# One transformer block on one core: value subtractions and filler stores on GpSimd, the convolution's last columns placed directly, pools reordered, the output bank in halves

## The chip, the cores and the metric

The kernel runs on one core of one Trainium2 chip. The metric is the device time of one execution in microseconds; the time before is the median of three runs. The engines are called by the profile's names: PE (TensorE, its weight loads as PEld), DVE (VectorE), ACT (ScalarE), POOL (GpSimd) and SP (SyncE, which here only issues DMAs). ACT and POOL can issue DMAs too; a DMA instruction stands in its engine's queue like any other.

## The reference

One layer of a hybrid encoder block for a sequence of 1024 tokens and 1024 channels, everything in float32:

```
h = rmsnorm(x, ln1_g) * (1 + sc1) + sh1          # sc1, sh1, ... from silu(c) @ ada_w + ada_b
q, k, v, cb, cc, cx, ga, gb = split(h @ w_in)
q, k = rmsnorm per head of 64 channels           # 16 heads
y_a = stick_breaking_attention(q, k, v)          # causal, blocks of 128 queries
      # A[t,s] = sigmoid(z_ts) * prod_{s<j<t} (1 - sigmoid(z_tj)),  z = q.k / 8,  s < t;  y_a = A @ v
y_b = cb * causal_dwconv3(cc * cx, conv_w)
merged = sigmoid(ga) * (y_a @ w_branch_a) + sigmoid(gb) * (y_b @ w_branch_b)
x = x + g1 * (merged @ w_out)
h = rmsnorm(x, ln2_g) * (1 + sc2) + sh2
x = x + g2 * ((silu(h @ w_gate) * (h @ w_up)) @ w_down)
```

## The kernel before

**Arithmetic.** Every float32 operand of a product is split into a high part (a copy by ACT into the type fp32r) and a low part (source minus high part, by DVE), and each product is three matmuls: high-high, high-low, low-high. The gate, FFN and down projections use a Strassen-like scheme of seven products.

**Stages.** Modulation and the first norm with the first value projection; keys; the gate and convolution inputs (`gates`, L478), whose results go to DRAM (`d_sga`, `d_sgb`, `d_y`); the attention stage, which the change is about (from about 578 to 1058 us); branch A's projection; output projection and second norm; FFN; down projection.

**The attention stage.** It interleaves two streams on the same engines.

*Attention* (`attention`, L815) walks 16 heads times 8 query blocks. A step does `att_scores` (z = q.k by two matmuls, L763 and L764; sigmoid by ACT into the tile pt, L765; running product by a DVE scan, L769); the step before it does `att_trans` (PE transposes, L784; high part by ACT, L787; low part by DVE, L788); three steps after the scores, every second step does `att_av` (L792: matmuls with the value tile into the bank `o`, L799 and L800; ACT adds the last value column, L804; DVE combines, L806; SP stores `d_ya`, L808). The product uses differences of neighbouring values: `att_load` (L698) loads q and k parts for one head and, for an even head, the value columns twice, once shifted by a row (`va` and `vb`, one buffer each, L712), always for the head after the current one. `att_dv` (L716) subtracts them on DVE (L720), copies the high part into `vt` by ACT (L723) and makes the low part by DVE (L724); `vt` has two buffers. `load_vlast` (L726) loads the last value rows, 16 heads in two goes, into a tile that shares the buffer of `va`; `turn_vlast` transposes it.

*Fillers* (`fillers`, L855) are matmul work that attention doesn't need at once: the value projection of heads 8 to 15 (two times eight items, stored to `d_v` by ACT, L875); 16 convolution items (m, n), m a block of 128 channels and n a half of the sequence (load `y` from `d_y`, L883; 24 matmuls; DVE multiplies, L889; high and low part, L892 and L893; ACT stores both to `d_yb`, L894 and L895); then all of `d_yb` is read back into four large buffers `yh`, `yl` (16 DMAs of 512 KB, L902 and L903); and 16 items of branch B's projection (load `sb` from `d_sgb`, L908; 24 matmuls; DVE multiplies, L915; ACT stores `d_mb`, L916). `y` and `mb` share three buffers, `sb` has two, the high and low parts two each.

**What sets the order.** The program is traced in Python and a scheduler then fixes the order of each engine's instructions from a simulated timeline, by priority (attention is traced under `tc.high_priority()`) and readiness. `fill` (L926) traces fillers in proportion to the attention traced so far. `tc.issue_after(ins)` adds an order without a wait: what is traced inside comes after `ins` on the engine of `ins`. Each engine works through its order strictly one after the other. `reuse_waits="tile"` means that a buffer is reused as soon as the tile in it is released. The large buffers `big()` (four) hold the normed input `hh`, `hl` and later `yh`, `yl`. Tile pools are opened and closed like a stack, so a pool's tiles lie where an earlier pool's tiles were, in the order in which their tags first appear; pool `phb` (L693) holds the attention tiles.

Of the kernel before, what the change touches and what calls it, by code (L numbers as in the profile page):

```python
# [8 lines left out]
F32 = mybir.dt.float32  # L9
F32R = mybir.dt.float32r  # L10
AF = mybir.ActivationFunctionType
ALU = mybir.AluOpType
# [4 lines left out]
P = 128  # L17
T = 1024
D = 1024
KT = D // P  # L20
H = 16
DH = 64
# [6 lines left out]
def block_kernel(tc, x, x_t, cols, ada_1, ada_2, ada_row, w_q, w_kv, w_v1, w_cg, w_a, w_b, w_o, w_g, w_u, w_d, out):  # L29
    nc = tc.nc  # L30
# [7 lines left out]
    def nm(s):  # L38
        uid[0] += 1
        return f"{s}_{uid[0]}"  # L40

    def big():
        return bigp.tile([P, KT, 512], F32R, tag="big", bufs=4, name=nm("big"))
# [24 lines left out]
    d_v = [drp.tile([T + 1, n], F32, name=f"d_v{n}_{e}") for e, n in enumerate((512, 256, 256))]  # L68
    d_yb = [[drp.tile([P, KT, 512], F32, name=f"d_yb{e}{n}") for n in range(2)] for e in range(2)]
    d_ya = [drp.tile([P, KT, 512], F32, name=f"d_ya{n}") for n in range(2)]  # L70
    d_sga = drp.tile([KT, P, T], F32, name="d_sga")
    d_sgb = drp.tile([KT, P, T], F32, name="d_sgb")
    d_y = drp.tile([KT, P, T], F32, name="d_y")
    d_mb = drp.tile([KT, P, T], F32, name="d_mb")
# [58 lines left out]
    def tt(eng, out, a, b, op):  # L133
        eng.tensor_tensor(out=out, in0=a, in1=b, op=op)  # L134
# [3 lines left out]
    pps = psA.enter_context(tc.tile_pool(name="psA", bufs=1, space=PSUM, reuse_waits="tile"))  # L138
# [123 lines left out]
                             start=True, stop=True)  # L262

    split_hi(0)
    hh = [big() for n in range(2)]
    hl = [big() for n in range(2)]

    def norm_x(k, *n):
        src = xt(k, *n)
# [159 lines left out]
    for cc in (1, 2):  # L429
        w = wq[4:] if cc == 1 else [load_w(w_kv[cc, j]) for j in range(4)]  # L430
# [255 lines left out]
    pps = psB.enter_context(tc.tile_pool(name="psB", bufs=1, space=PSUM, reuse_waits="tile"))  # L686
# [4 lines left out]
    fq = fqpool.enter_context(tc.tile_pool(name="phg", bufs=1, side="right", reuse_waits="tile"))  # L691
    s3 = ExitStack()
    bp = s3.enter_context(tc.tile_pool(name="phb", bufs=1, reuse_waits="tile"))  # L693

    NPT = 5
    pts = [ptp.tile([P, D], F32, name=f"pt{j}") for j in range(NPT)]

# [18 lines left out]
    def att_dv(h):  # L716

        va, vb = vab
        if h % 2 == 0:
            tt(nc.vector, vb, vb, va, ALU.subtract)  # L720
        dv = vb[:, :, h % 2 * DH:h % 2 * DH + DH]
        vt = vts[h] = bp.tile([P, KT, P], F32R, tag="vt", bufs=2, name=nm("vt"))
        nc.scalar.activation(vt[:, :, :DH], dv, AF.Copy)  # L723
        tt(nc.vector, vt[:, :, DH:], dv, vt[:, :, :DH].bitcast(F32), ALU.subtract)  # L724

    def load_vlast(e):  # L726

        vl = bp.tile([8, 512], F32, tag="va", bufs=1, name=nm("vl"))
        for d, c in (((0, 0),), ((1, 0), (2, 256)))[e]:
            nc.sync.dma_start(vl[:, c:c + d_v[d].shape[1]], d_v[d][1:].rearrange("(i p) d -> i p d", p=P)[:, P - 1])  # L730
        return vl
# [10 lines left out]
    lastz = [None]  # L742
    lastld = [None]
    npt = [0]
    ats = {}
    ptof = {}

# [44 lines left out]
    def att_av(h, g):  # L792
        pr, e0 = h // 2, (h % 2) * DH
        vt = vts[h]
        o = pps.tile([P, 256], F32, tag="o", bufs=1, name=nm("o"))
        for j in range(2 * g + 2):
            c0 = P if j == 2 * g + 1 else 0
            th, tl = ats[h, g, j // 4]
            nc.tensor.matmul(o[:, c0:], vt[:, j, :], th[:, j % 4, c0:], start=(j == 0), stop=False)  # L799
            lastav[0] = nc.tensor.matmul(o[:, c0:], vt[:, j, :], tl[:, j % 4, c0:], start=False, stop=(j == 2 * g + 1))  # L800
        tmp = bp.tile([DH, 256], F32, tag="otmp", bufs=1, name=nm("otmp"))
        yv = bp.tile([DH, 256], F32, tag="oy", bufs=2, name=nm("oy"))
        for e in range(2):
            nc.scalar.activation(tmp[:, e * P:(e + 1) * P], o[:DH, e * P:(e + 1) * P], AF.Identity,  # L804
                                 bias=vlast[:, h, 2 * g + e:2 * g + e + 1])
        nc.vector.tensor_tensor(out=yv, in0=o[DH:], in1=tmp, op=ALU.add)  # L806
        hf, c0 = g // 2, (g % 2) * 256
        nc.sync.dma_start(d_ya[hf][e0:e0 + DH, pr, c0:c0 + 256], yv)  # L808
        yield (2 * g + 2) * 0.22

    NZ, NTR, NPJ, DAV, KQ = 2, 3, 2, 3, 2
# [30 lines left out]
    def load_ch(src):  # L842
        raw = g_raw(src)
        return g_split(raw[:, :512]), g_split(raw[:, 512:])
# [10 lines left out]
    def fillers():  # L855
        for e in range(2):
            w = []
            for j in range(2):
                with tc.issue_after(lastld[0].ins) if e else ExitStack():
                    raw = g_raw(w_v1[e, j])  # L860
                w += [g_split(raw[:, :512]), g_split(raw[:, 512:])]
            for i in range(8):
                n, t0 = i // 4, (i % 4) * P
                ps = ps_f()[:, :256]
                for k in range(KT):
                    if k == 4:
                        yield 1.3
                    wh, wl = (v[:, (k % 2) * 256:(k % 2) * 256 + 256] for v in w[k // 2])
                    sh, sl = hh[n][:, k, t0:t0 + P], hl[n][:, k, t0:t0 + P]
                    nc.tensor.matmul(ps, sh, wh, start=(k == 0), stop=False)  # L870
                    nc.tensor.matmul(ps, sh, wl, start=False, stop=False)
                    nc.tensor.matmul(ps, sl, wh, start=False, stop=(k == KT - 1))
                vs = fq.tile([P, 256], F32, tag=("ybh", "ybl")[i % 2], bufs=2, name=nm("vs1"))
                nc.scalar.activation(vs, ps, AF.Copy)
                nc.scalar.dma_start(d_v[1 + e][1 + i * P:1 + (i + 1) * P], vs)  # L875
                yield 1.3
        cb_w = {}
        for m, n in [(m, n) for m in range(KT - 2) for n in range(2)] + [(m, n) for n in range(2) for m in (KT - 2, KT - 1)]:
            if n == 0:
                cb_w[m] = load_ch(w_cg[0, m])  # L880
            w = cb_w[m]
            y = fp.tile([P, 512], F32, tag="st", bufs=3, name=nm("cy"))
            nc.sync.dma_start(y, d_y[m, :, n * 512:(n + 1) * 512])  # L883
            ps = ps_f()
            for kk in range(0, KT, KQ):
                if kk:
                    yield 0.65 * KQ
                mm_ch(ps, w, hh[n], hl[n], kk, kk + KQ)
            nc.vector.tensor_tensor(out=y, in0=ps, in1=y, op=ALU.mult)  # L889
            yh = fq.tile([P, 512], F32R, tag="ybh", bufs=2, name=nm("ybh"))  # L890
            yl = fq.tile([P, 512], F32R, tag="ybl", bufs=2, name=nm("ybl"))
            nc.scalar.activation(yh, y, AF.Copy)  # L892
            nc.vector.tensor_tensor(out=yl, in0=y, in1=yh.bitcast(F32), op=ALU.subtract)  # L893
            nc.scalar.dma_start(d_yb[0][n][:, m, :], yh.bitcast(F32))  # L894
            nc.scalar.dma_start(d_yb[1][n][:, m, :], yl.bitcast(F32))  # L895
            yield 0.65 * KQ
        yh, yl = [], []
        for n in range(2):
            yh.append(big())
            yl.append(big())  # L900
            for k in range(0, KT, 2):
                nc.sync.dma_start(yh[n][:, k:k + 2].bitcast(F32), d_yb[0][n][:, k:k + 2])  # L902
                nc.sync.dma_start(yl[n][:, k:k + 2].bitcast(F32), d_yb[1][n][:, k:k + 2])  # L903
        for m in range(KT):
            w = load_ch(w_b[m])
            for n in range(2):
                sb = fp.tile([P, 512], F32, tag="sgi", bufs=2, name=nm("sgi"))
                nc.sync.dma_start(sb, d_sgb[m, :, n * 512:(n + 1) * 512])  # L908
                ps = ps_f()
                for kk in range(0, KT, KQ):  # L910
                    if kk:
                        yield 0.65 * KQ
                    mm_ch(ps, w, yh[n], yl[n], kk, kk + KQ)
                mb = fp.tile([P, 512], F32, tag="st", bufs=3, name=nm("mb"))
                nc.vector.tensor_tensor(out=mb, in0=ps, in1=sb, op=ALU.mult)  # L915
                nc.scalar.dma_start(d_mb[m, :, n * 512:(n + 1) * 512], mb)  # L916
                yield 0.65 * KQ

    FILL = 2.5 * 16 * 5.2
# [14 lines left out]
    with tc.high_priority():  # L934
        vl = load_vlast(0)
# [38 lines left out]
    for n in range(2):  # L974
        for k in range(KT):
            yr = fp.tile([P, 512], F32, tag="yr", bufs=2, name=nm("yr"))
            nc.sync.dma_start(yr, d_ya[n][:, k, :])
            tag, bufs = slots[n * KT + k]
# [6 lines left out]
    for m in range(KT):  # L985
        if m == KT - 1:
            split_wo(g_raw(w_o[0]), cpa, 1, ("c00", "c10", "c01", "c11"))
        w = load_ch(w_a[m])
        for n in range(2):
            sa = fp.tile([P, 512], F32, tag="sgi", bufs=2, name=nm("sgi"))  # L990
            nc.sync.dma_start(sa, d_sga[m, :, n * 512:(n + 1) * 512])
            mb = fp.tile([P, 512], F32, tag="st", bufs=3, name=nm("mb"))
# [17 lines left out]
    pps = psD.enter_context(tc.tile_pool(name="psD", bufs=1, space=PSUM, reuse_waits="tile"))  # L1010
# [404 lines left out]
    vt = [e2.tile([P, 512], F32, name=f"vt{t}") for t in range(4)]  # L1415
# [101 lines left out]
    for t in range(4):  # L1517
        for e, c, ps in ((nc.sync, slice(0, 256), pa[3]), (nc.scalar, slice(256, 512), pa[7])) if t == 3 else (
                (nc.sync, slice(0, 512), pa[t]),):
            nc.vector.scalar_tensor_tensor(out=vt[t][:, c], in0=ps[:, :c.stop - c.start], scalar=gmod[:, 1, t:t + 1],  # L1520
                                           in1=u2t[t][:, c], op0=ALU.mult, op1=ALU.add)
# [60 lines left out]
```

## Time and profile before

| | before |
|---|---|
| time, median of 3 runs | 1875.63 us (1875.41 to 1878.0) |
| the profiled execution | 1874.59 us, span 1872.5 us |
| mean granted TensorE clock | 0.991 |
| busy: PE / PEld / DVE / ACT / POOL | 1813.7 / 1503.2 / 1343.1 / 777.7 / 415.5 us |
| chain that ended last | PE 76%, DVE 11%, DMA 6%, issue 3%, ACT 2%, POOL 1% |
| DMA bytes | 351.94 MB, mean 188 GB/s |

The span is the time from the first to the last instruction of the profiled execution. "Busy" is the time in which an engine had an instruction under way; a row of the profile names the line, the engine, the operation, the tile written and the tiles read, the count, the busy time, the mean duration in ns, and the time that the engine stood idle before these instructions with what ended it. A name with a q (ACTq, SPq) is the engine's queue: there DMAs and semaphore waits appear.

### The profile page before, as it was taken

What the parts mean: (1) busy time and instruction counts of PE and PEld (TensorE: products, weight loads), DVE (VectorE), ACT (ScalarE), POOL (GpSimd) and SP (SyncE); (2) the same over time, 40 slices, a digit from 0 to 9 for tenths busy, and PEclk for the clock granted to TensorE, in tenths of its full rate; (3) what the DMA queues carried; (4) which work ended last, traced back from release to release, by engine and by line L of the source; (5) the groups of instructions that cost most, each with busy time, mean ns of one, the idle gap of its engine ahead of it and who ended that gap; (6) DMA issues with size and microseconds to landing.
All of it is one profiled execution on the core that took longest, in us unless ns stands there. A gap on an engine that the chain in (4) does not pass through costs nothing.

```text
span 1872.5 us, 24605 instructions
## 1 busy us (share of the span) xinstructions
PE 1813.7 (97%) x8765; PEld 1503.2 (80%) x8765; DVE 1343.1 (72%) x1896; ACT 777.7 (42%) x1462; POOL 415.5 (22%) x292
## 2 busy tenths in 40 slices
PE   7999999999999999988999999999999999999999
PEld 4787778887788988877888788877888888888787
DVE  6873877779953878877788554489997778643953
ACT  4342553333333656555556322244444344422320
POOL 1043328323420000000000001336554545300000
PEclk9999999999999999998999999999999999999999
DMA  9598452228638575667663544514454344299776
GB/s 388 198 309 307 162 176 77 76 93 292 227 123 251 134 189 163 185 191 250 168 167 95 195 131 158 169 57 169 147 191 147 135 154 172 102 347 327 247 234 216
DMA packets 154112, 351.94 MB, mean 188 GB/s; under 512 B 15211, under 2 KB 54397, under 8 KB 151814
## 3 DMA queue, kind: packets, MB, share of 16 engines
q1 hardware_dynamic: 96336, 239.54, 40.3%
q10 hardware_dynamic: 56646, 107.16, 15.7%
q0 software_dynamic: 1008, 3.67, 0.5%
q8 instruction: 70, 1.15, 0.3%
q14 instruction: 52, 0.43, 0.1%
HBM read 240.73 MB, written 109.58 MB: 187 GB/s over the span
## 4 chain that ended last, share of the span: by engine, by line
PE 76%; DVE 11%; DMA 6%; issue 3%; ACT 2%; POOL 1%; SPq 0%; ACTq 0%; DVEq 0%; POOLq 0%
PE e L129 6%; PE e L130 6%; PE e L131 6%; PE pj L129 5%; PE pj L292 5%; PE pj L130 5%; PE pj L131 5%; PE pj L851 4%; PE pj L852 4%; PE pj L853 4%; PE e L1425 3%; PE e L1423 3%; PE e L1424 3%; PE tr L784 3%; PE o L800 2%
## 5 line engine op out<-in xcount | busy, mean ns | idle before, releaser
L769 DVE TENSOR_TENSOR_SCAN pt<-pt,mk 128x128 f32<-128x128 f32 (+7 forms) x128 | 172.1, 1350 | 51.1 <-ACT pt L765 50.3
L134 POOL TENSOR_TENSOR acc<-acc,sq 128x512 f32<-128x512 f32 x13 | 17.2, 1326 | 646.7 <-ACT sq L1075 646.7
L765 ACT ACTIVATE pt<-z,rq 128x512 f32<-128x512 f32 (+1 forms) x192 | 107.7, 579 | 100.9 <-PE z L764 47.5
L134 DVE TENSOR_TENSOR wlo<-raw,whi 128x512 fp32r<-128x512 f32 x148 | 114.1, 782 | 43.3 <-ACT whi L468 32.4
L129 PE MATMUL e<-big,whi 128*128 128x512 f32 x352 | 137.6, 391 | 1.2 <-DVE c L134 1.1
L130 PE MATMUL e<-big,whi 128*128 128x512 f32 x352 | 137.3, 390 | 0.0
L131 PE MATMUL e<-big,wlo 128*128 128x512 f32 x352 | 137.1, 390 | 0.0
L134 DVE TENSOR_TENSOR c<-e,c 128x512 f32<-128x512 f32 x154 | 102.9, 682 | 43.0 <-PE e L131 42.9
L129 PE MATMUL pj<-big,whi 128*128 128x512 f32 x320 | 125.9, 393 | 4.2 <-ACT whi L468 2.7
L130 PE MATMUL pj<-big,whi 128*128 128x512 f32 x320 | 125.5, 392 | 0.0
L131 PE MATMUL pj<-big,wlo 128*128 128x512 f32 x320 | 124.9, 392 | 0.0
L1423 PE MATMUL e<-f,whi 128*128 128x512 f32 (+1 forms) x319 | 122.0, 383 | 1.6 <-DMA f<-d_f 0.9
L134 POOL TENSOR_TENSOR ws<-raw,raw 128x512 f32<-128x512 f32 x40 | 60.0, 1501 | 285.4 <-DMA raw<-w_cg 136.2
L1424 PE MATMUL e<-f,whi 128*128 128x512 f32 (+1 forms) x319 | 121.9, 382 | 0.0
L134 DVE TENSOR_TENSOR c<-pj,c 128x512 f32<-128x512 f32 x140 | 93.3, 683 | 38.7 <-PE pj L131 37.6
L1425 PE MATMUL e<-f,wlo 128*128 128x512 f32 (+1 forms) x319 | 117.1, 383 | 2.6 <-DVE wlo L1031 2.6
L292 PE MATMUL pj<-whi,big 128*128 128x512 f32 x352 | 109.9, 398 | 4.0 <-ACT big L275 4.0
L468 ACT ACTIVATE whi<-raw 128x512 fp32r<-128x512 f32 x116 | 72.4, 628 | 94.5 <-PE pj L130 43.4
L788 DVE TENSOR_TENSOR atl<-tr,ath 128x512 fp32r<-128x512 f32 (+1 forms) x192 | 99.7, 549 | 12.7 <-ACT ath L787 11.0
L787 ACT ACTIVATE ath<-tr 128x512 fp32r<-128x512 f32 (+1 forms) x192 | 86.9, 489 | 49.7 <-PE o L799 30.7
L784 PE MATMUL tr<-dm,pt 128*128 128x128 f32 x576 | 97.0, 278 | 10.6 <-DVE atl L788 10.3
L129 PE MATMUL e<-rh,whi 128*128 128x512 f32 x264 | 102.9, 390 | 2.5 <-DVE c L134 2.5
(255 smaller groups left out, 4993.0 us busy)
## 6 DMA issues: line engine op xcount, KB each, us to landing
f<-d_f SPq DMA_DIRECT2D x77, 512.0 KB, 4.3
d_f<-fs ACTq DMA_DIRECT2D x70, 512.0 KB, 2.7
raw<-w_cg SPq DMA_DIRECT2D x40, 512.0 KB, 3.6
raw<-w_g SPq DMA_DIRECT2D x24, 512.0 KB, 3.7
raw<-w_u SPq DMA_DIRECT2D x24, 512.0 KB, 3.4
ad<-ada ACTq DMA_DIRECT2D x19, 512.0 KB, 4.6
ada<-ada SPq DMA_DIRECT2D x8, 1024.0 KB, 10.4
d_t<-ts SPq DMA_DIRECT2D x16, 512.0 KB, 5.5
```

The lines of the kernel that those rows point to most:

```text
L129: nc.tensor.matmul(ps, wh[:, k, :], fh[:, k, :], start=(k == 0), stop=False)
L130: nc.tensor.matmul(ps, wh[:, k, :], fl[:, k, :], start=False, stop=False)
L131: nc.tensor.matmul(ps, wl[:, k, :], fh[:, k, :], start=False, stop=(k == 3))
L134: eng.tensor_tensor(out=out, in0=a, in1=b, op=op)
L292: nc.tensor.matmul(ps, a, b, start=(k == 0 and q == 0), stop=(k == KT - 1 and q == 2))
L765: nc.scalar.activation(pt[:, off + s0:off + s0 + m], z[:, :m], AF.Sigmoid, scale=rq[:, 1, i, h:h + 1])
L769: nc.vector.tensor_tensor_scan(out=pt[:, rev], data0=pt[:, rev], data1=mk[:, rev], initial=1.0, op0=ALU.mult, op1=ALU.max)
L784: nc.tensor.transpose(tr[:, j * P:(j + 1) * P], pt[:, off + (b0 + j) * P:off + (b0 + j + 1) * P], ident)
L788: nc.vector.tensor_tensor(out=tl[:, :nb, c0:c0 + P], in0=src, in1=th[:, :nb, c0:c0 + P].bitcast(F32), op=ALU.subtract)
L1423: nc.tensor.matmul(o, wh, f[:, 0, c], start=(j == 0), stop=False)
L1424: nc.tensor.matmul(o, wh, f[:, 1, c], start=False, stop=False)
L1425: nc.tensor.matmul(o, wl, f[:, 0, c], start=False, stop=(j == NJ - 1))
```

## The change

1. `att_dv`: both subtractions go from DVE to POOL; ACT's copy between them stays.
2. The stores of the fillers (`d_v`, `d_yb`, `d_mb`) are issued by POOL's queue instead of ACT's.
3. The last two channel blocks of the convolution are written straight into `yh`, `yl`; only six of eight blocks are stored and read back, and the read-back of half n is traced right after its item (7, n).
4. Branch B's items run in the order (0,0), (1,0), (0,1), (1,1), (2,0), (2,1), ...
5. The loads of `y`, `yh`, `yl` and `sb` come on SP after the last value load traced so far (`lastld`).
6. `load_vlast` has a buffer of its own. The pool `phb` begins with the tags ath, atl and vt (one tile each is taken and not used).
7. The bank `o` becomes one tile of two halves that `att_av` uses in turn.
8. The large buffers are taken in the order hh0, hl0, hh1, hl1 instead of hh0, hh1, hl0, hl1.

```diff
-    hh = [big() for n in range(2)]
-    hl = [big() for n in range(2)]
+    hh, hl = [], []
+    for n in range(2):
+        hh.append(big())
+        hl.append(big())
...
+    for tag, bufs in (("ath", 3), ("atl", 3), ("vt", 2)):
+        bp.tile([P, KT, P], F32R, tag=tag, bufs=bufs, name=nm(tag))
...
         if h % 2 == 0:
-            tt(nc.vector, vb, vb, va, ALU.subtract)
+            tt(nc.gpsimd, vb, vb, va, ALU.subtract)
         dv = vb[:, :, h % 2 * DH:h % 2 * DH + DH]
         vt = vts[h] = bp.tile([P, KT, P], F32R, tag="vt", bufs=2, name=nm("vt"))
         nc.scalar.activation(vt[:, :, :DH], dv, AF.Copy)
-        tt(nc.vector, vt[:, :, DH:], dv, vt[:, :, :DH].bitcast(F32), ALU.subtract)
+        tt(nc.gpsimd, vt[:, :, DH:], dv, vt[:, :, :DH].bitcast(F32), ALU.subtract)
...
-        vl = bp.tile([8, 512], F32, tag="va", bufs=1, name=nm("vl"))
+        vl = bp.tile([8, 512], F32, tag="vl", bufs=1, name=nm("vl"))
...
+    obank = pps.tile([P, 2, 256], F32, name="obank")
...
-        o = pps.tile([P, 256], F32, tag="o", bufs=1, name=nm("o"))
+        o = obank[:, g % 2]
...
-                nc.scalar.dma_start(d_v[1 + e][1 + i * P:1 + (i + 1) * P], vs)
+                nc.gpsimd.dma_start(d_v[1 + e][1 + i * P:1 + (i + 1) * P], vs)
                 yield 1.3
         cb_w = {}
+        yh, yl, ylate = [], [], []
         for m, n in [(m, n) for m in range(KT - 2) for n in range(2)] + [(m, n) for n in range(2) for m in (KT - 2, KT - 1)]:
...
-            nc.sync.dma_start(y, d_y[m, :, n * 512:(n + 1) * 512])
+            with tc.issue_after(lastld[0].ins):
+                nc.sync.dma_start(y, d_y[m, :, n * 512:(n + 1) * 512])
...
             nc.vector.tensor_tensor(out=y, in0=ps, in1=y, op=ALU.mult)
+            if m >= KT - 2:
+                ylate.append(y)
+                if m == KT - 1:
+                    yh.append(big())
+                    yl.append(big())
+                    with tc.issue_after(lastld[0].ins):
+                        for k in range(0, KT - 2, 2):
+                            nc.sync.dma_start(yh[n][:, k:k + 2].bitcast(F32), d_yb[0][n][:, k:k + 2])
+                            nc.sync.dma_start(yl[n][:, k:k + 2].bitcast(F32), d_yb[1][n][:, k:k + 2])
+                    for k in (KT - 2, KT - 1):
+                        y = ylate.pop(0)
+                        nc.scalar.activation(yh[n][:, k], y, AF.Copy)
+                        tt(nc.vector, yl[n][:, k], y, yh[n][:, k].bitcast(F32), ALU.subtract)
+                yield 0.65 * KQ
+                continue
...
-            nc.scalar.dma_start(d_yb[0][n][:, m, :], yh.bitcast(F32))
-            nc.scalar.dma_start(d_yb[1][n][:, m, :], yl.bitcast(F32))
+            nc.gpsimd.dma_start(d_yb[0][n][:, m, :], yh_.bitcast(F32))
+            nc.gpsimd.dma_start(d_yb[1][n][:, m, :], yl_.bitcast(F32))
             yield 0.65 * KQ
-        yh, yl = [], []
-        for n in range(2):
-            yh.append(big())
-            yl.append(big())
-            for k in range(0, KT, 2):
-                nc.sync.dma_start(yh[n][:, k:k + 2].bitcast(F32), d_yb[0][n][:, k:k + 2])
-                nc.sync.dma_start(yl[n][:, k:k + 2].bitcast(F32), d_yb[1][n][:, k:k + 2])
-        for m in range(KT):
-            w = load_ch(w_b[m])
-            for n in range(2):
+        order = [(0, 0), (1, 0), (0, 1), (1, 1)] + [(m, n) for m in range(2, KT) for n in range(2)]
+        wb = {}
+        for m, n in order:
+            if n == 0:
+                wb[m] = load_ch(w_b[m])
+            w = wb[m]
+            for _ in range(1):
                 sb = fp.tile([P, 512], F32, tag="sgi", bufs=2, name=nm("sgi"))
-                nc.sync.dma_start(sb, d_sgb[m, :, n * 512:(n + 1) * 512])
+                with tc.issue_after(lastld[0].ins):
+                    nc.sync.dma_start(sb, d_sgb[m, :, n * 512:(n + 1) * 512])
...
-                nc.scalar.dma_start(d_mb[m, :, n * 512:(n + 1) * 512], mb)
+                nc.gpsimd.dma_start(d_mb[m, :, n * 512:(n + 1) * 512], mb)
```

More of the change, by code (lines that the diff above doesn't have):

```diff
@@ L889, in fillers @@
             nc.vector.tensor_tensor(out=y, in0=ps, in1=y, op=ALU.mult)
[L890 to L893, printed above, removed]
-            nc.scalar.dma_start(d_yb[0][n][:, m, :], yh.bitcast(F32))
-            nc.scalar.dma_start(d_yb[1][n][:, m, :], yl.bitcast(F32))
@@ new lines, in fillers @@
+            yh_ = fq.tile([P, 512], F32R, tag="ybh", bufs=2, name=nm("ybh"))
+            yl_ = fq.tile([P, 512], F32R, tag="ybl", bufs=2, name=nm("ybl"))
+            nc.scalar.activation(yh_, y, AF.Copy)
+            nc.vector.tensor_tensor(out=yl_, in0=y, in1=yh_.bitcast(F32), op=ALU.subtract)
+            nc.gpsimd.dma_start(d_yb[0][n][:, m, :], yh_.bitcast(F32))
+            nc.gpsimd.dma_start(d_yb[1][n][:, m, :], yl_.bitcast(F32))
+            yield 0.65 * KQ
+        order = [(0, 0), (1, 0), (0, 1), (1, 1)] + [(m, n) for m in range(2, KT) for n in range(2)]
```

## The prediction

> **What bounds the kernel now.** I read the page first, for the busy shares and the chain; then stretches of 10 to 30 us over the attention stage (578 to 1058 us), to find where TensorE stops; then the chain, the waits and the queues' timelines at each stop.
>
> ```profile
> span 1872.5 us, 24605 instructions
> PE 1813.7 (97%) x8765; PEld 1503.2 (80%) x8765; DVE 1343.1 (72%) x1896; ACT 777.7 (42%) x1462; POOL 415.5 (22%) x292
> ```
> TensorE sets the time: 1813.7 of 1872.5 us. An edit elsewhere pays only where TensorE stands still. The profiled execution took 1874.6 us, 2.1 above its span and 1.0 below the median of 1875.63.
>
> ```profile
> 590.00:610.00 20.00, 16.22 (x108) 14.37 (x106) 12.14 (x17) 10.01 (x25) 0.00 (x0) 0.91 0.96 265
> 660.00:670.00 10.00, 7.79 (x50) 6.76 (x50) 9.47 (x14) 5.59 (x13) 0.00 (x0) 1.00 1.02 243
> 780.00:800.00 20.00, 17.49 (x98) 14.78 (x97) 14.10 (x19) 10.46 (x23) 0.00 (x0) 0.91 0.46 141
> 830.00:850.00 20.00, 13.97 (x68) 11.92 (x67) 13.50 (x20) 6.62 (x14) 0.00 (x0) 0.83 1.04 336
> 870.00:890.00 20.00, 16.92 (x96) 14.47 (x94) 12.05 (x15) 9.78 (x22) 0.00 (x0) 0.91 0.66 205
> 900.00:920.00 20.00, 17.27 (x105) 15.49 (x104) 16.13 (x22) 10.58 (x25) 0.00 (x0) 0.91 0.47 161
> 1030.00:1060.00 30.00, 27.22 (x146) 22.45 (x145) 15.68 (x28) 11.86 (x27) 0.00 (x0) 1.00 0.60 193
> 578.00:1058.00 480.00, 454.67 (x2782) 397.85 (x2780) 371.80 (x511) 269.44 (x616) 0.00 (x0) 0.98 0.63 178
> ```
> Columns: stretch, length, busy time of PE, PEld, DVE, ACT, POOL, then granted clock, DMA share, GB/s. The last row gives the prize: 480.00 - 454.67 = 25.3 us of TensorE idle, with POOL wholly free and DVE at 77%. The first seven rows hold 23.1 of it: 3.78, 2.21, 2.51, 6.03, 3.08, 2.73 and 2.78. After five of these stops the granted clock is low. Busy time times (1 - clock) is 1.5 + 1.6 + 2.4 + 1.5 + 1.6 = 8.6 us more, lost because TensorE stopped.
>
> ```profile
> 593.31 9.55 DMA raw<-w_v
> 602.94 0.33 ACTq L875
> 603.31 0.38 ACT pt L765
> 837.65 5.75 DMA d_ya<-oy
> 843.47 0.33 ACTq L895
> 843.84 0.70 ACT pt L765
> 778.90 6.83 DMA va<-d_v
> 861.02 10.27 DMA skh<-d_k
> 871.37 5.58 DMA d_ya<-oy
> ```
> Three mechanisms show in the chain. (a) ACT's own stores (L875, L895) are held until an older, unrelated transfer has landed (a load of w_v, a store of d_ya that SP issued), and the sigmoid L765 queued behind them on ACT is late; TensorE's next scores wait for it. (b) DVE stands at the subtraction of the two shifted value tiles until va or vb has landed. (c) At 861 to 877 loads of skh and a store are slow while the convolution's columns are read back (L902, L903).
>
> **The change part by part.**
>
> *Filler stores from ACT to POOL's queue* (16 of d_v, 16 of d_mb, and 24 of the 32 of d_yb; the other 8 vanish). Both stops of mechanism (a) start at one of them: 3.78 at 590:610 and 6.03 at 830:850. No store is left on ACT to hold the sigmoid. The second I count whole (6.0), the first below. POOL pays this:
>
> ```profile
> L1362 POOL DMA_DIRECT2D d_f<-fs x7 | 4.0, 566 | 46.2 <-DVE fs L134 46.1
> d_f<-fs ACTq DMA_DIRECT2D x70, 512.0 KB, 2.7
> d_f<-fs POOLq DMA_DIRECT2D x7, 512.0 KB, 7.4
> ```
> 56 x 0.57 = 32 us of POOL, which is idle. Landing from POOL took 7.4 against 2.7 us from ACT for twice these bytes. A source tile has two buffers (three for mb), and a filler item comes about every 12 us (16 + 16 whole and 16 half items in 480 us), so 7.4 is covered by some 24; without that cover ACT or DVE would stand for the difference.
>
> *Value subtractions from DVE to POOL.*
>
> ```profile
> L134 DVE TENSOR_TENSOR vb<-vb,va 128x1024 f32<-128x1024 f32 x8 | 9.8, 1225 | 29.2 <-DMA vb<-d_v 18.0 <-issue 6.1 <-DMA va<-d_v 5.1
> L134 DVE TENSOR_TENSOR vt<-vb,vt 128x512 fp32r<-128x512 f32 x16 | 10.7, 677 | 0.0
> 660.44 1.23 DVE L134 TENSOR_TENSOR vb<-vb,va 128x1024 f32<-128x1024 f32 x1 [3.52 <-issue]
> 785.75 1.23 DVE L134 TENSOR_TENSOR vb<-vb,va 128x1024 f32<-128x1024 f32 x1 [5.12 <-DMA va<-d_v]
> 900.23 1.23 DVE L134 TENSOR_TENSOR vb<-vb,va 128x1024 f32<-128x1024 f32 x1 [2.52 <-DMA vb<-d_v]
> 683.91 0.65 ACT L723 ACTIVATE vt<-vb 128x512 fp32r<-128x512 f32 x1
> L134 POOL TENSOR_TENSOR ws<-raw,raw 128x512 f32<-128x512 f32 x40 | 60.0, 1501 | 285.4 <-DMA raw<-w_cg 136.2 <-DMA raw<-w_q 37.7 <-DVE wlo L1031 29.6
> ```
> DVE is freed of 9.8 + 10.7 = 20.5 us of work and of 29.2 us of standing in front of it. The waits at 660, 786 and 900 lie on the stops 2.21, 2.51 and 2.73. The wait now falls on POOL, where only stores queue behind it (5.1 us at most, inside the cover above). ACT's copy L723 needs the difference, but it comes 23 us after it (683.91 against 660.44) since it waits for a free vt, so it does not take the wait over. At 900 the chain goes on through ACT and a scan, so I count half: 2.21 + 2.51 + 1.4 = 6.1. The separate vl buffer belongs here: today a vl tile holds va's single buffer until it is transposed, and va is first requested at 778.90. On POOL the work is 8 x 3.0 (two 512-wide by its row) + 16 x 1.5 = 48 us; at the start ACT's first copy waits for it directly, 3.0 - 1.2 = 1.8 us later than today.
>
> What POOL does to DVE:
>
> ```profile
> L1031 DVE TENSOR_TENSOR wlo<-ws,whi 128x512 fp32r<-128x512 f32 x73 | 74.8, 1035 | 13.5 <-ACT whi L1030 13.4
> L1031 DVE TENSOR_TENSOR wlo<-raw,whi 128x512 fp32r<-128x512 f32 x52 | 42.2, 814 | 0.2
> L134 DVE TENSOR_TENSOR wlo<-raw,whi 128x512 fp32r<-128x512 f32 x38 | 25.6, 677 | 0.8 <-ACT whi L468 0.8
> 1300.00:1400.00 100.00, 100.00 (x443) 82.82 (x442) 94.71 (x118) 46.72 (x81) 50.90 (x34) 1.00 0.48 175
> L769 DVE TENSOR_TENSOR_SCAN pt<-pt,mk 128x128 f32<-128x128 f32 (+7 forms) x128 | 172.1, 1350 | 51.1 <-ACT pt L765 50.3
> ```
> The same split takes 677 ns in attention (POOL idle) and (74.8 + 42.2) / 125 = 936 ns where POOL is half busy, so about 0.55 us is lost per us of overlap. In attention the scans and splits with two SBUF inputs are about half of DVE's time: 48 x 0.5 x 0.55 = 13 us, at most 26 if all overlaps. Against 20.5 + 29.2 given up, DVE has less to do or 5.5 us more in a stage with 108 us of slack; cost taken 0, bound 5.5.
>
> On this the Trainium skill speaks against the move: GPSIMD Engine Reference, section 4.1, gives elementwise work on a tile to VectorE because two-input operations are about twice as slow on GpSimd, and its section 8 names contention with DVE instructions of two SBUF inputs. By that page alone the move would count as a loss; both of its effects agree with the rows above (1501 against 677 ns, 936 against 677 ns).
>
> *Convolution's last columns into place, order (0,0) (1,0) (0,1) (1,1).* Eight stores of 256 KB and four of the sixteen 512 KB read-backs vanish, 4 MB at a place with DMA share 1.04. The second half's read-back is now covered by two items of the first half (24 us). Of the 3.08 us at 870:890 I take 2.0; bounds 0 and 3.1.
>
> *Loads of y and sb held behind the last value load* (the new ordering on SP): they no longer go ahead of head loads. Nothing in the trace shows them late; what they may cost is the second rival. I allow one stop of the size seen, 3.0 us; bounds 0 and the rival.
>
> *Order of pool phb.* Today the tiles loaded first lie where the gates' tiles were:
>
> ```profile
> SPq L730 <- PE pj L131: 7.7, 1, 7.7
> SPq L706 <- DMA d_sga<-c: 4.0, 1, 4.0
> ```
> Placed behind ath, atl and vt, they fall on tiles of earlier gates, so head 0's loads can start up to 11 us sooner, into a stretch that is DMA-bound (0.96). With the stores gone from ACT I take half of its 3.78: 1.9, bounds 0 and 3.8, less the 1.8 above.
>
> *Output bank in halves.*
>
> ```profile
> PE o L799 <- DVE oy L806: 3.8, 6, 1.7
> PEld o L799 <- DVE oy L806: 2.1, 2, 1.9
> ```
> If halves were independent this would go: up to 5.9 us. I take 0: both halves are one tile in one bank, and I expect the wait to be kept on the whole tile. The Trainium skill, PSUM — Partial Sum Buffer, section "PSUM bank collisions raise a hardware error", asks for guarding by bank and not by address; by it the gain is 0, by the rows alone 5.9.
>
> *Order of hh and hl:* the same four buffers, all free long before they are written; 0.
>
> *Clock:* TensorE idle falls by 6.0 + 6.1 + 2.0 + 1.9 = 16.0 of the 20.3 us of the first six stops; the same share of the 8.6 is 6.8.
>
> Sum: 16.0 + 6.8 - 1.8 - 3.0 = 18.0 us. 1874.6 - 18.0 = 1856.6 for an execution like the profiled one; from the median, 1857.6. The times below are from the median.
>
> **The rivals.**
>
> 1. *The waits move on.* SP keeps its own waits for older transfers, and DMA stays saturated at 590 and 830; a stop avoided on ACT returns at the next in-order queue. For it: share 1.04 at 830, and d_ya behind skh at 861 to 877. Against it: the stores were on ACT's path and on POOL nobody waits for them. Only the 6.1 of the value waits stays: about 1869.5.
>
> 2. *Slower: y and sb arrive late.* They now queue on SP behind vb's load, and that waits for the last use of vb:
>
> ```profile
> SPq L712 <- DVE vt L134: 26.8, 6, 6.7
> DMA to landing us min/median/max: 4.0/6.5/9.0
> ```
> DVE would stand at L889 or L915 as it stood at vb, in front of the scans. A wait of 3.5 + 5.1 + 2.5 = 11.1 us on DVE gave 7.45 of TensorE idle, 0.67 each. If the first load in each of 15 heads comes 3 us late, 15 x 3 x 0.67 = 30 against 18: about 1888. It decides from 1.8 us a head. Against it: an item lasts 12 us and three buffers let its load go ahead.
>
> 3. *All of it.* The first six stops go whole, with the clock: 20.3 + 8.6 = 28.9, about 1847.
>
> **How the numbers follow.** Forecast 0.60. Its own range is 1851 to 1867: down without the allowed stop (3.0) and with the upper bounds at the start and the read-back (1.9 + 1.1), up with both at 0 (1.9 + 2.0) and DVE's 5.5. Rival 1 0.20, rival 2 0.13, rival 3 0.07. About 0.2% (3.8 us) is what a measurement here can tell from no change. Faster than 1871.9: 0.60 + 0.07 + half of rival 1 = 0.77. Within: 0.10, from rival 1. Slower: 0.13. The range runs from 1846 (below rival 3) to 1874; above it lie rival 2 and a little of rival 1.
>
> **What would show it.** Right: no wait of ACT's sigmoid on a transfer; DVE with no row vb<-vb,va and POOL with some 48 us in attention; TensorE idle over the stage near 25.3 - 16.0 = 9 us instead of 25.3; no stop at the w_b items' start. Wrong: DVE waiting at L889's or L915's successor for a DMA; ACT's L723 or ybh waiting for POOL; scans much above 1350 ns; idle near 25 in other places.

## The result and the profile after

| | before | after |
|---|---|---|
| time, median | 1875.52 us (1874.27 to 1878.0) | 1844.72 us (1843.81 to 1848.69) |
| ratio, 95% interval | | 0.9838 [0.9821, 0.9856] |
| profiled execution, span | 1874.59, 1872.5 us | 1848.69, 1846.9 us |

The change makes the kernel faster by 30.4 us (0.0162 of 1875.5; 27.0 to 33.6). Forecast were 18.0, with a range from 1846 to 1874 us: the direction held, the size did not. The profiled execution after is the slowest of its four, 4.0 us above the median.

The page of the changed kernel, engines and two queues:

```profile
span 1846.9 us, 24631 instructions
PE 1805.1 (98%) x8765; PEld 1498.8 (81%) x8765; DVE 1335.5 (72%) x1872; ACT 778.0 (42%) x1462; POOL 496.8 (27%) x372
q10 hardware_dynamic: 47430, 92.48, 13.7%
q0 software_dynamic: 4976, 16.26, 2.3%
```

Stretches of the changed kernel in the columns of the prediction (stretch, length, PE, PEld, DVE, ACT, POOL, granted clock, DMA share, GB/s):

```profile
590.00:610.00 20.00, 19.55 (x154) 18.73 (x153) 16.64 (x19) 14.98 (x34) 10.44 (x8) 1.00 0.84 231
830.00:850.00 20.00, 18.54 (x109) 15.56 (x108) 16.45 (x22) 11.42 (x26) 3.17 (x2) 1.00 0.86 260
870.00:890.00 20.00, 19.99 (x124) 17.40 (x123) 18.44 (x25) 12.24 (x28) 4.59 (x4) 1.00 0.71 198
585.00:1000.00 415.00, 411.56 (x2596) 364.20 (x2595) 353.54 (x466) 258.92 (x592) 80.40 (x76) 1.00 0.65 180
```

The same 415 us of the kernel before:

```profile
585.00:1000.00 415.00, 392.89 (x2413) 344.75 (x2412) 330.30 (x450) 238.85 (x547) 0.00 (x0) 0.98 0.65 183
```

Most of the stops are gone: TensorE idles 3.4 us in these 415 instead of 22.1, at a granted clock of 1.00 instead of 0.98. The count of matmuls says the same: 2596 against 2413 in the same stretch, 183 more, and 183 x 415 / 2596 = 29.3 us, if a matmul takes the same time on average. Idle (18.7) and the clock lost in the five stretches of the prediction (8.6) make 27.3 of it; where the rest lies is not shown.

The gain lies in the attention stage. Start of the running product (scan, DVE) in the traces, us:

| scan | before | stores alone | subtractions alone | convolution alone | stores and subtractions | the three | changed kernel |
|---|---|---|---|---|---|---|---|
| first, head 0 | 592.2 | 587.8 | 587.8 | 590.2 | 587.8 | 588.5 | 588.1 |
| first, head 8 | 804.4 | 801.9 | 797.1 | 801.5 | 789.8 | 793.2 | 790.0 |
| first, head 10 | 865.5 | 855.6 | 856.1 | 859.3 | 843.9 | 847.5 | 845.7 |
| first, head 12 | 927.1 | 917.3 | 916.5 | 916.4 | 905.2 | 897.3 | 895.4 |
| last | 1026.5 | 1017.1 | 1016.7 | 1016.3 | 1005.5 | 997.6 | 994.9 |

At the last scan the changed kernel is 31.6 us ahead. Its span is only 25.6 us shorter: this execution loses 6 us behind the attention stage, at a granted clock of 0.99 there instead of 1.00. The first row differs by 2 us for the convolution's part too, whose work comes much later, so 2 us between two traces are no evidence of a part.

### The profile page after: what moved, and what is told of

It reads as the page before. It is cut to its first block, busy times and chain, and to the rows that moved or that the text cites. A ratio compares the mean times of both kernels' runs of the same rounds, so it can differ in the third digit from the quotient of the medians.

```text
span 1846.9 us, 24631 instructions
## 1 busy us (share of the span) xinstructions
PE 1805.1 (98%) x8765; PEld 1498.8 (81%) x8765; DVE 1335.5 (72%) x1872; ACT 778.0 (42%) x1462; POOL 496.8 (27%) x372
## 3 DMA queue, kind: packets, MB, share of 16 engines
q10 hardware_dynamic: 47430, 92.48, 13.7%
## 4 chain that ended last, share of the span: by engine, by line
PE 78%; DVE 11%; DMA 5%; issue 3%; ACT 2%; POOL 1%; SPq 0%; ACTq 0%; DVEq 0%; POOLq 0%
PE e L129 6%; PE e L130 6%; PE e L131 6%; PE pj L129 5%; PE pj L294 5%; PE pj L130 5%; PE pj L131 5%; PE pj L857 4%; PE pj L859 4%; PE pj L858 4%; PE e L1446 3%; PE e L1444 3%; PE e L1445 3%; PE tr L790 3%; PE z L769 2%
## 5 line engine op out<-in xcount | busy, mean ns | idle before, releaser
L775 DVE TENSOR_TENSOR_SCAN pt<-pt,mk 128x128 f32<-128x128 f32 (+7 forms) x128 | 177.1, 1392 | 50.1 <-ACT pt L771 49.4
L134 DVE TENSOR_TENSOR wlo<-raw,whi 128x512 fp32r<-128x512 f32 x148 | 121.5, 832 | 48.2 <-ACT whi L470 34.0
L771 ACT ACTIVATE pt<-z,rq 128x512 f32<-128x512 f32 (+2 forms) x192 | 107.8, 579 | 80.8 <-PE z L770 50.2
L129 PE MATMUL pj<-big,whi 128*128 128x512 f32 x320 | 125.8, 393 | 4.6 <-ACT whi L470 3.3
L130 PE MATMUL pj<-big,whi 128*128 128x512 f32 x320 | 125.3, 391 | 0.0
L857 PE MATMUL pj<-big,whi 128*128 128x512 f32 x256 | 103.7, 405 | 0.0
L130 PE MATMUL e<-rl,whi 128*128 128x512 f32 x264 | 103.2, 391 | 0.0
```

The costliest lines, as they stand in the source:

```text
L129: nc.tensor.matmul(ps, wh[:, k, :], fh[:, k, :], start=(k == 0), stop=False)
L130: nc.tensor.matmul(ps, wh[:, k, :], fl[:, k, :], start=False, stop=False)
L771: nc.scalar.activation(pt[:, off + s0:off + s0 + m], z[:, :m], AF.Sigmoid, scale=rq[:, 1, i, h:h + 1])
L775: nc.vector.tensor_tensor_scan(out=pt[:, rev], data0=pt[:, rev], data1=mk[:, rev], initial=1.0, op0=ALU.mult, op1=ALU.max)
L857: nc.tensor.matmul(ps, wh, rh_, start=(k == 0), stop=False)
```

## The experiments

Times are medians; us faster than before are worked out from the ratio and 1875.5.

| kernel | median us | ratio, 95% interval | faster by |
|---|---|---|---|
| a_stores: before + stores on POOL | 1867.16 | 0.9959 [0.9943, 0.9974] | 7.7 |
| a_subs: before + subtractions on POOL | 1866.76 | 0.9951 [0.9937, 0.9965] | 9.2 |
| a_conv: before + convolution's part | 1861.80 | 0.9926 [0.9911, 0.9941] | 13.9 |
| a_stsub: stores and subtractions | 1854.40 | 0.9888 [0.9873, 0.9903] | 21.0 |
| a_three: all three | 1842.48 | 0.9828 [0.9813, 0.9844] | 32.3 |
| a_direct: columns into place only | 1862.16 | 0.9931 [0.9918, 0.9944] | 12.9 |
| a_reord: item order only | 1872.05 | 0.9987 [0.9978, 0.9996] | 2.4 |
| a_vbonly: first subtraction only | 1870.24 | 0.9975 [0.9964, 0.9987] | 4.7 |
| u_order: changed, loads not held back | 1845.04 | 0.9839 [0.9821, 0.9857] | 30.2 |
| u_pool: changed, old pool order | 1846.70 | 0.9856 [0.9839, 0.9872] | 27.0 |
| u_bank: changed, old bank, old hh order | 1846.82 | 0.9849 [0.9834, 0.9864] | 28.3 |
| u_subs: changed, subtractions on DVE | 1851.37 | 0.9879 [0.9859, 0.9899] | 22.7 |
| u_stores: changed, stores on ACT | 1855.98 | 0.9887 [0.9870, 0.9905] | 21.2 |
| u_sp: changed, stores on SP | 1849.14 | 0.9867 [0.9846, 0.9887] | 24.9 |
| three_tail30 | 1855.21 | 0.9898 [0.9884, 0.9911] | 19.1 |
| three_tail15 | 1849.43 | 0.9871 [0.9851, 0.9891] | 24.2 |
| three_tail10 | 1846.00 | 0.9854 [0.9833, 0.9874] | 27.4 |

**Each part alone.** `a_stores`:

```diff
-                nc.scalar.dma_start(d_v[1 + e][1 + i * P:1 + (i + 1) * P], vs)
+                nc.gpsimd.dma_start(d_v[1 + e][1 + i * P:1 + (i + 1) * P], vs)
...
-            nc.scalar.dma_start(d_yb[0][n][:, m, :], yh.bitcast(F32))
-            nc.scalar.dma_start(d_yb[1][n][:, m, :], yl.bitcast(F32))
+            nc.gpsimd.dma_start(d_yb[0][n][:, m, :], yh.bitcast(F32))
+            nc.gpsimd.dma_start(d_yb[1][n][:, m, :], yl.bitcast(F32))
...
-                nc.scalar.dma_start(d_mb[m, :, n * 512:(n + 1) * 512], mb)
+                nc.gpsimd.dma_start(d_mb[m, :, n * 512:(n + 1) * 512], mb)
```

> The kernel before with one part of the change: the filler stores are issued by POOL's queue instead of ACT's. Theory 1 (the stops are separate and each part removes its own): the stops at 590:610 and 830:850 go with their lost clock, 3.78 + 6.03 + 1.5 + 2.4 = 13.7 us, so 1861.8; DVE's rows at vb stay near 29 us, the stops at 660, 786 and 900 remain. Theory 2 (the stops are one congestion of the shared transfer lanes, and the stores are its cause): most of the whole gain of 30.8 comes with this part alone, 1850 or less. Theory 3 (a stop avoided on ACT returns elsewhere, only the parts together help): within 4 us of before.

`a_subs`:

```diff
-            tt(nc.vector, vb, vb, va, ALU.subtract)
+            tt(nc.gpsimd, vb, vb, va, ALU.subtract)
...
-        tt(nc.vector, vt[:, :, DH:], dv, vt[:, :, :DH].bitcast(F32), ALU.subtract)
+        tt(nc.gpsimd, vt[:, :, DH:], dv, vt[:, :, :DH].bitcast(F32), ALU.subtract)
```

> The kernel before with one part of the change: both value subtractions on POOL. Theory 1: the stops at 660, 786 and 900 go with their clock, 7.45 + 1.6 + 1.6 = 10.6 us, so 1864.9; ACT's sigmoid still waits for transfers behind its stores. Theory 2: under 5 us, 1870 or more, as DVE's waits are only a symptom. Theory 3: within 4 us of before.

`a_conv` is the convolution and branch B block of the change's diff, with the stores left on `nc.scalar` and the loads without `tc.issue_after`; `a_stsub` is both diffs above.

> The kernel before with one part of the change: the convolution's last two blocks straight into place, only six blocks stored and read back, and branch B's items in the order (0,0) (1,0) (0,1) (1,1); stores stay on ACT, loads are not held back. Theory 1: the stop at 870:890 goes with its clock, 3.08 + 1.5 = 4.6 us, so 1870.9; if the 4 MB less also empties 830:850, another 6.03 + 2.4, so 1862.5. Theory 2: under 3 us. Theory 3: within 4 us of before.

> The kernel before with two parts of the change: filler stores on POOL and value subtractions on POOL, nothing else. Theory 1: the sum of the two alone, 13.7 + 10.6 = 24.3 us, so 1851.2. Theory 2: little more than the stores alone, within 4 us of them. Theory 3: clearly more than the sum of the two alone.

Measured: 7.7, 9.2 and 13.9; their sum 30.8 is the whole (30.4), and 21.0 for the pair lies above its sum of 16.9, but the intervals overlap. Theory 2 falls in all four, and theory 3 for the single parts; for the pair, more than the sum is not shown. Theory 1 holds for the addition, but not for all of its sizes: stores gave less than 13.7, subtractions about the 10.6, and the convolution three times 4.6, close to the 13.0 of its second branch (both stretches emptied). Two stretches each, of a_stores, then a_conv, then a_stsub:

```profile
830.00:850.00 20.00, 18.80 (x116) 15.91 (x115) 18.86 (x29) 12.71 (x28) 1.62 (x3) 1.00 1.05 341
855.00:875.00 20.00, 13.10 (x69) 11.34 (x68) 10.80 (x18) 7.19 (x18) 0.54 (x1) 0.84 0.97 301
```

```profile
830.00:850.00 20.00, 17.19 (x107) 14.41 (x106) 16.12 (x26) 10.93 (x25) 0.00 (x0) 1.00 0.93 246
860.00:880.00 20.00, 14.96 (x86) 12.71 (x85) 9.70 (x14) 6.97 (x18) 0.00 (x0) 0.91 0.74 192
```

```profile
830.00:850.00 20.00, 19.44 (x112) 16.09 (x111) 16.21 (x22) 10.72 (x24) 4.46 (x4) 1.00 1.02 347
850.00:870.00 20.00, 12.72 (x65) 10.81 (x64) 8.21 (x12) 6.90 (x17) 0.00 (x0) 0.83 0.62 182
```

The 6.03 us stop at 830:850 shrinks to 1.2 with the stores' part and to 2.8 with the convolution's part alone. But the next thing in line then stops TensorE: 6.9 us at 855:875 in a_stores, 5.0 at 860:880 in a_conv, 7.3 at 850:870 in a_stsub. In a_conv it is again ACT, whose store of d_mb (L931) is held until a load of sqt has landed, with the sigmoid behind it; in a_stsub it is SP. The two chains, a_conv's first:

```profile
856.83 12.02 DMA sqt<-d_q
868.93 0.33 ACTq L931
869.30 0.70 ACT pt L765
```

```profile
837.34 10.53 DMA big<-d_yb
847.88 0.02 SPq L808
847.93 11.15 DMA d_ya<-oy
859.18 0.44 DVE oy L806
859.75 0.55 PE o L799
```

By the second chain, attention's own 64 KB store of y_a is held on SP until a read-back has landed (10.53 us), then takes 11.15 us itself; DVE has no free oy, and the output bank is not emptied. A chain of the same kind stood in the prediction for the kernel before, at 861 to 877 (a load of skh, then d_ya), with a stop of 3.08. That it was smaller there because other stops had already taken the time is the likely reason, not a shown one.

With all three parts little of this is left, as two stretches of a_three show:

```profile
840.00:860.00 20.00, 19.45 (x117) 16.76 (x116) 16.48 (x26) 9.97 (x25) 0.56 (x1) 1.00 0.94 255
860.00:880.00 20.00, 20.00 (x116) 17.01 (x116) 19.20 (x24) 12.11 (x27) 6.25 (x4) 1.00 0.84 218
```

The table of scans says where each part acts. From head 8 to head 10 the kernel before takes 61.1 us, with the stores alone 53.7: that is nearly all of their 7.7. From head 10 to head 12 it takes 61.6 us, and 61.7, 60.4 and 61.3 with the stores, the subtractions and the pair; with the three it takes 49.8. The 11.5 us between the pair and the three lie wholly there, and 11.3 were measured. The convolution's part alone takes 3.3 us from the first of these stretches and 4.5 from the second; its trace, that of the slowest of six executions, shows less than the 13.9 by the medians. In it the two stretches are not empty (2.8 and 5.0 us of idle above), so that 13.9 comes near the 13.0 of the second branch does not bear this branch out.

**The parts left out.** `a_three` is the pair with a_conv's block; `u_order`, `u_pool` and `u_bank` are the changed kernel with one small part taken back:

```diff
 # u_order (three places)
-            with tc.issue_after(lastld[0].ins):
+            if True:
 # u_pool
-    for tag, bufs in (("ath", 3), ("atl", 3), ("vt", 2)):
-        bp.tile([P, KT, P], F32R, tag=tag, bufs=bufs, name=nm(tag))
 # u_bank
-        o = obank[:, g % 2]
+        o = pps.tile([P, 256], F32, tag="o", bufs=1, name=nm("o"))
...
+    hh = [big() for n in range(2)]
+    hl = [big() for n in range(2)]
```

> The kernel before with the stores, the subtractions and the convolution's part; without the held-back loads, the separate vl buffer, the pool order, the output bank and the order of hh and hl. Theory 1 (the three mechanisms carry the change, the other parts are worth nothing): within 3 us of the changed kernel, 1844 to 1848. Theory 2 (the other parts carry a share): 5 us or more above it, 1850 or more.

> The changed kernel without the ordering of the loads of y, yh, yl and sb on SP behind the last value load. If these loads, going ahead, delayed head loads as at 590 before: 3 us or more slower than the changed kernel. Rival 2 of the prediction in small (held-back loads cost something): faster than it by 2 us or more. Theory 1: within 2 us of it.

> The changed kernel without the three tiles taken at the head of pool phb (its tags in the old order). The prediction's step on the pool gives +1.9 us, at most +3.8. The first scores started at 586.4 us before and 586.2 after, so theory 1 now expects no difference: within 2 us of the changed kernel.

> The changed kernel with the output bank o as one buffer per product again and the large buffers in the old order. Theory 1 (both worth 0, the two halves are guarded as one bank): within 2 us of the changed kernel, and PE and PEld still wait for DVE's oy about as often in both. If halves are independent: up to 5.9 us slower.

The three mechanisms alone give all of it: a_three and the changed kernel agree within their intervals. Taking back the ordering costs 0.2 us; pool order (3.4) and bank with hh order (2.1) stay inside the intervals, so neither a small gain nor none is shown for them. The separate vl buffer was taken back only in a_three, with all the rest. The waits of the first matmul on the output bank, of the changed kernel and of u_bank:

```profile
PEld obank L805: 2.3, 3
PE obank L805: 1.9, 2
```

```profile
PE o L802: 2.0, 3
PEld o L802: 1.9, 1
```

4.2 us in five waits against 3.9 in four: the two halves are still waited for as one.

**Inside two of the parts.** `a_reord` puts the change's `order` loop on the kernel before and reads all of d_yb back; `a_direct` is a_conv with the old loop; `a_vbonly` is the first line of a_subs' diff; `three_tail30` is a_three with

```diff
-    HEAD, TAIL = 10, 20.0
+    HEAD, TAIL = 10, 30.0
```

> The kernel before with branch B's items in the order (0,0) (1,0) (0,1) (1,1), all of d_yb still stored and read back. The convolution's part alone gave 13.9 us by the medians. Theory R (the hole is the second half's read-back, which blocks item (0,1)): the order gives most of it, 9 to 14 us, 1861 to 1866. Theory D (the traffic and the wait of the read-back for the last stores): the order alone gives under 4 us.

> The kernel before with the last two blocks straight into place and the read-back of each half right after its last item, branch B's items in the old order. Theory R: under 5 us, as item (0,1) still comes second and waits. Theory D: 9 to 14 us, 1861 to 1866.

> The kernel before with only the first subtraction (vb, 8 of 24) on POOL; DVE keeps the 16 of vt, 10.7 us. If the wait in front of the subtraction is what costs: 7 to 10 us, as both subtractions gave (9.2). If DVE's work costs: about half of it, 3 to 5 us.

> The kernel with stores, subtractions and the convolution's part, and the filler work kept for after the last attention product raised from 20 to 30 (the kernel's own unit). TensorE idles some 4 us between the last attention products and branch A's first (stores and reloads of d_ya). If more filler work covers the reloads: 1 to 3 us below the 1842.5 of the kernel without it. If the attention stage lacks these fillers: slower by 2 us or more.

Theory D holds: the direct columns give 12.9 of the 13.9, the order 2.4. In a_reord DVE multiplies branch B's second item at 883.1 us instead of 893.7, so the hole in the fillers closes, and nearly nothing is won. So it is the stores and read-backs that vanish, and not the hole: among the eight dropped stores (items (6, n) and (7, n)) is the ACTq L895 at 843.47 that ended the 6.03 us stop. That the read-back is traced earlier is not it either: its first piece is issued at 828.0 us in a_direct and at 826.5 in the kernel before. Stores and read-backs were not taken apart.

The first subtraction alone gives 4.7, about half of both (9.2), but the intervals nearly meet (2.4 to 6.8 and 6.6 to 11.8). That DVE's 10.7 us of work on vt are the other half is not shown. In the traces a_vbonly is 0.6 us behind a_subs at the first scan of head 10 and 5.9 behind at head 12's. In between it has a stop of TensorE of 2.85 us at 899.8 that a_subs hasn't, after a weight split of DVE that took 2.75 us, against 0.68 us for the usual one, beside POOL's subtraction:

```profile
898.16 2.75 DVE L134 TENSOR_TENSOR wlo<-raw,whi 128x512 fp32r<-128x512 f32 x1
897.98 2.38 POOL L134 TENSOR_TENSOR vb<-vb,va 128x1024 f32<-128x1024 f32 x1 [72.46 <-DMA vb<-d_v]
```

`three_tail30` went the other way, 13 us slower, which opened the question of the last runs.

**What sets the stage's pace.** `three_tail10` and `three_tail15` set TAIL to 10.0 and 15.0 in a_three. `u_subs` and `u_stores` are the first two diffs taken back in the changed kernel; in `u_sp` its stores read `nc.sync` for `nc.gpsimd`.

> The kernel with stores, subtractions and the convolution's part, with 10 units of filler work kept for after the last attention product instead of 20 (30 cost 12.7 us). If attention's own chain sets the stage's length, the 10 units that move into it are free: 6 to 12 us below 1842.5, less what branch A's reloads then leave bare on TensorE (some 4 us). If TensorE's work sets it: within 3 us of 1842.5, or slower by the bare reloads.

> The same with 15 units. Chain: 3 to 6 us below 1842.5. TensorE: within 2 us of it.

> The changed kernel with both value subtractions back on DVE. The part alone on the kernel before gave 9.2 us. If parts add: 8 to 11 us slower than the changed kernel. If DVE's work counts for more once the other stops are gone: 15 us or more. If it was only the waits for va and vb behind ACT's stores: under 4 us.

> The changed kernel with the filler stores issued by SP instead of POOL. If the gain is only that ACT is free of them: within 3 us of the changed kernel. If SP's loads, then queued behind stores that wait for results, come late: 4 us or more slower, with DVE or PE waiting for q, k or value loads.

> The changed kernel with the filler stores back on ACT's queue. If the parts add: about 8 us slower than the changed kernel (ratio to before 0.988), with ACT's sigmoid held again behind stores that wait for older transfers. If the stop at 830:850 was all they removed, and the convolution's part removes it too: within 3 us of the changed kernel. If the stores' waits are what is left of the sums above 31: 10 us or more.

More filler work inside the stage is not free: 27.4 (TAIL 10) and 24.2 us (15) below before, against 32.3 at 20, where attention's chain alone would have given 6 to 12 and 3 to 6 more. The last attention product starts at 1022.0 and 1019.7 us instead of 1012.9. So attention's chain alone does not set the length, and TensorE's work counts. Less filler work (30) does not shorten the stage either: the last attention product starts at 1014.2 us. TensorE idles 10.6 us in 585:1000 against 5.2 in a_three, at a clock of 0.99 against 1.00, and the fillers that were kept back run afterwards: what follows the last product takes 843.0 us instead of 830.6. Why the stage with fewer fillers did not get shorter stays open. Every such setting also gives a new order of all instructions, so these three runs show only that none of them improves upon 20.

From the other side the parts add again: taking the subtractions back costs 7.7 us, the stores 9.2. With the stores on ACT in an otherwise changed kernel the old wait is back, as ACT's waits in u_stores show:

```profile
ACT pt L771 <- DMA skl<-d_k: 11.3, 1, 11.3
```

`u_sp` is 5.5 us behind the changed kernel by the ratios and 4.4 by the medians, but the intervals overlap, and the traces show no difference in the stage (last scan at 994.7 against 994.9): whether POOL is better than SP stays open.

## Why the prediction was wrong

By its own steps:

- **Which mechanisms: right.** (a), (b) and (c) carry the change. In the changed kernel no sigmoid of ACT ends its wait on a transfer, DVE has no subtraction of vb, and of the stops of the first six stretches 1.5 us at 830:850 and 0.45 at 590:610 are left. TensorE idles 6.5 us over the stage (578:1027); forecast were 9.
- **Stores: 7.9 us and 3.4 of clock forecast, 11.3 together; 7.7 alone and 9.2 taken back measured.** Too high by 2 to 4 us. The wait that went is the one named: between heads 8 and 10, where the stop of 6.0 and its 2.4 of clock lay, the stores alone take off 7.4 us.
- **Subtractions: 6.1 + 2.6 - 1.8 = 6.9 forecast, 9.2 alone and 7.7 taken back measured.** Near enough. Priced were only the waits, and DVE's work was put at 0 on the ground of slack; whether the work counts, a_vbonly does not settle. The charge of 1.8 us at the start shows in a_subs (ACT's first copy at 594.15 us instead of 592.31), but there DVE no longer stands 15.16 us in front of vb before the first scan, which comes 4.4 us earlier. In a_stores it does too, as the new order puts this scan ahead of the subtraction.
- **Convolution: 2.0 us and 0.8 of clock forecast, 13.9 alone and 11.3 on top of the other two measured.** This is the step that failed: "Of the 3.08 us at 870:890 I take 2.0; bounds 0 and 3.1". The mechanism (c) was right and its term was too small: of the 12.4 us that the forecast lacks (30.4 - 18.0), 11.3 - 2.8 = 8.5 are here, and 3.0 are the next point. The upper bound was the stop seen in the trace of before, and the 6.03 us at 830:850 were booked to the stores alone ("The second I count whole (6.0)"), though the convolution's part alone shrinks them too, to 2.8. With the two other parts in place the waits around the read-back stop TensorE for longer than in the kernel before: in a_stsub 7.3 us idle at 850:870 and 12.72 x 0.17 = 2.2 us of clock, 9.5 of the 11.3, and in a_three 0.6 us at 840:860 and none at 860:880. No row of before shows a stop of that size for the read-back; only the chain (skh 10.27 us, d_ya 5.58 us) shows the slow transfers.
- **Rival 1 was right in part.** In a_stores, a_conv and a_stsub the next in-order queue stops TensorE for longer (6.9, 5.0 and 7.3 us) than in the kernel before (3.08); only with all three parts it does not. But the parts kept their gains, and the rival's 1869.5 did not come.
- **The allowed stop of 3.0 us for held-back loads: 0.** u_order differs by 0.2, with intervals of some 3 us to either side. Rival 2 did not happen: DVE waits for no load of y or sb.
- **Halves and discounts.** The stop at 590 was counted half and went nearly whole (0.45 left). Rival 3, every stop with its clock, came to 28.9 us against 30.4 measured, and had 0.07. That its sum is so near is in good part luck: by the same rule the stores would give 13.7 (7.7 and 9.2 measured), the subtractions 10.6 (9.2 and 7.7) and the convolution 4.6 (13.9 and 11.3), and the errors cancel.
- **Pool order: the step failed, at a cost that the runs can't tell from none.** The loads of head 0 did not start up to 11 us sooner (the first at 572.1 us against 572.3). SP's waits in the changed kernel:

```profile
SPq L710 <- PE pj L131: 5.1, 1, 5.1
SPq L711 <- DMA d_sga<-c: 4.1, 1, 4.1
```

  The first scores came at 586.2 us against 586.4.
- **POOL's price: right in the sum, not in its form.** The subtractions on POOL, from the changed kernel, and the scans with POOL (changed) and without (u_subs):

```profile
L134 POOL TENSOR_TENSOR vt<-vb,vt 128x512 fp32r<-128x512 f32 x16 | 31.7, 1984 | 99.7 <-ACT vt L728 99.7
L134 POOL TENSOR_TENSOR vb<-vb,va 128x1024 f32<-128x1024 f32 x8 | 20.8, 2602 | 33.4 <-issue 24.2 <-DMA vb<-d_v 9.2
L775 DVE TENSOR_TENSOR_SCAN pt<-pt,mk 128x128 f32<-128x128 f32 (+7 forms) x128 | 177.1, 1392 | 50.1 <-ACT pt L771 49.4
L134 DVE TENSOR_TENSOR wlo<-raw,whi 128x512 fp32r<-128x512 f32 x38 | 33.3, 879 | 1.8 <-ACT whi L470 1.8
```

```profile
L775 DVE TENSOR_TENSOR_SCAN pt<-pt,mk 128x128 f32<-128x128 f32 (+7 forms) x128 | 171.6, 1349 | 42.0 <-ACT pt L771 40.9
```

  52.5 us against 48 forecast. The scans lose 5.5 us, the 38 weight splits 33.3 - 25.6 = 7.7, together 13.2; forecast were 13. The forecast took a loss in proportion to the overlap. The trace shows single instructions that stand beside POOL's: five scans and four splits of DVE are slower than their kind by 12.9 us together, and the others by next to nothing. One of them:

```profile
921.01 2.70 DVE L134 TENSOR_TENSOR wlo<-raw,whi 128x512 fp32r<-128x512 f32 x1
920.78 2.38 POOL L134 TENSOR_TENSOR vb<-vb,va 128x1024 f32<-128x1024 f32 x1 [3.44 <-issue]
```

  The split, begun 0.23 us after POOL's subtraction, ends 0.55 us after it. So the 13 came out right partly by luck, and one such instruction in the wrong place makes a stop, as at 899.8 in a_vbonly. The contention with two-input DVE instructions that the Trainium skill names (GPSIMD Engine Reference, section 8) shows in these rows. Its advice against elementwise work there (section 4.1) does not decide this case: DVE stood in front of the subtraction longer (29.2 us) than it loses to POOL (13.2).

## What to carry to other kernels

A stop in the trace is not the worth of its cause. When several in-order queues wait on slow transfers, the stop is booked to the one that ends last, and the others can wait behind it unseen: look in the chain for transfers that take longer than usual (here skh 10.27 us against a median of 6.2, d_ya 5.58 against 2.9), and do not take the stop beside them for the upper bound of an edit that takes traffic away. How many us such transfers are worth, only the runs told: leave the parts out one at a time.

A DMA issue belongs on a queue where nobody waits behind it. That a small store that frees a buffer of the critical loop should not stand behind large loads follows from the chain of a_stsub, but no run moved that store. And a total that comes out right is no proof of its terms: the undiscounted sum of 28.9 was near only because an excess on the stores and a lack on the convolution cancelled.

## What the runs showed that was not expected

A 64 KB store of y_a took 11.15 us in the chain of a_stsub, behind the read-back of 512 KB pieces; its median from issue to landing in the kernel before:

```profile
d_ya<-oy SPq DMA_DIRECT2D x64, 64.0 KB, 2.9
```

The 1984 ns of POOL's subtraction of vt are a mean of two kinds. Its row by min/median/max in ns:

```profile
L134 POOL TENSOR_TENSOR vt<-vb,vt x16: 1287/2244/2655, 592.8 to 967.0; 128x512 fp32r<-128x512 f32 x16
```

Seven of the sixteen took 1.29 to 1.30 us, the other nine 2.2 us or more, and all nine began while a scan of DVE had over 1 us to go. So the delay goes both ways: POOL also stands beside DVE.

Stores of 256 KB from POOL's queue landed in 4.7 to 5.7 us by the medians of the changed kernel, below the 7.4 that the 512 KB rows of before had suggested:

```profile
d_mb<-mb POOLq DMA_DIRECT2D x16, 256.0 KB, 4.7
d_yb<-ybl POOLq DMA_DIRECT2D x12, 256.0 KB, 5.7
```
